# A two-layer hybrid attention and mLSTM inference step on one core: the order of the work set anew, and eight two-input operations on the other of VectorE and GpSimd

## Chip, cores and metric

One core of one Trainium2 chip runs the whole step. The metric is the device time of one execution in microseconds (us), lower is better; the kernel before takes 915.91 us (median of 3 runs, 913.62 to 922.15).

## The reference, cut to what matters

560 tokens (32 of a sample stream, 16 meta tokens, 512 of a prompt) go through two layers. All is in float32. Per layer:

```python
h = rmsnorm(x, norm_g)
q, k, v, z_a, qi, ki, wi, u, v_m, o_m, z_m, ig, fg = split_cols(h @ w_in)
q, k = rope(rmsnorm(q)), rope(rmsnorm(k))                # 8 heads x 64
score = (relu(qi.ki) * wi).sum(heads); keep the top 128  # sparse attention
attn = softmax(q.k of the kept keys) @ v
c = silu(causal_conv(u)); qm, km = c @ wq_m, c @ wk_m    # mLSTM, 4 heads x 128
num, den = mlstm_chunks(qm, km, v_m, ig, log_sigmoid(fg))
h_m = rmsnorm(num / den)
mixed = [attn * silu(z_a), (sigmoid(o_m) * h_m + skip * c) * silu(z_m)]
y = x + mixed @ w_out
```

Results are `y`, the keys, values and indexer keys of both streams, and the mLSTM and conv states.

## The kernel before, in words

Activations lie with features on the partitions and the 560 tokens along the free axis, cut in two halves of 304 and 256 (`HALVES`). Each weight piece (128 or 256 columns wide) is loaded in 256 KB parts by `load_piece` (L498) and split into a high and a low part (`whi` by ScalarE, L472; `wlo = wraw - whi`, L509); the activations are split likewise, and every product is three TensorE matmuls: high by high (L554), low by high (L555), high by low (L556) in `mm_feat`, and the same in `mm_tok` (L531 to L533). So a 128-wide projection is 48 matmuls. PSUM has four pools of two buffers each: `pj` for projections, `sc`, `tp` and `pv` for the rest. A third projection half can therefore start only when the drain of the first (the instruction that reads PSUM) is done. A drain has a priority of its own, stage "D".

The work of a layer is a list of steps, each a letter and an index:

- I and the KI piece (the head of `layer`): indexer queries and keys; J ropes and splits the indexer key (`rope` L599 to L607; splits at L713, L714). R ropes and splits the indexer queries (`stack_split` L564, its subtraction is L569), X0 to X3 (`index_pair`, matmuls L765) and N (`index_sample`, L789, L793) make the scores, T0 to T3 (`top`) find the top 128 with max and match_replace on VectorE (L821, L822).
- U0 to U3 (`conv`): projection, drains L889 to L891 on VectorE, convolution. M0, M1: the mLSTM's values. E: gates. F0 to F4 (`ml_front`, L929 to L946), C0 to C4 (`ml_mid`, L958 to L974, each after the one before), B0 to B4 (`ml_back`): the mLSTM by chunks of tokens.
- Q0 to Q3, K0 to K3 (`qk`): projection, rope, the sums of squares (L1030), a chain of small operations on GpSimd for the reciprocal root (`rsqrt` L580, L586 to L591; L1040), and for K a transpose on TensorE (L1049), a trip through DRAM (`kscr`), a scaling (L1059) and the split (L569). V0, V1 (`proj_v`): attention values. Apj (`attend`; Ap4 is `attend_last`): attention of head pair p for token block j, with scores L1166, transposes L1183 and L1192, values L1200. It needs Qp, Kp, both V and, for block j, the masks of T.
- O, Z, G (`gate_o`, `gate_z`): gates, with drains L1218 and L1238. S0 to S7 (`split`, subtraction L1253): split of the mixed features. Y0 to Y7: output projection; in layer 0 it also makes layer 1's split input and its sum of squares (`take` L615, the add is L634). `norm` (L639) turns the sums into `rrow`, with which every drain multiplies.

What an engine runs is set by a scheduler: every instruction has a priority, the ready instruction with the lowest goes first, and the compiled program then runs in that fixed order on each engine. A step's priority is

```python
off[0] = 500 * OPT[f"pos{l}"] * i + 10000 * SHIFT[l].get(t, 0)
with prio(l * 1000000 + PR[l][stage] + off[0]): ...
```

where `i` is the step's position in `STEPS[l]`. `OPT` names, per place and layer, the engine of an operation: `E(site, l)` is VectorE for 0 and GpSimd for 1. All DMAs are issued by SyncE.

Of the kernel before, what the change touches and what calls it, by code (L numbers as in the profile page):

```python
# [53 lines left out]
for _n in WORDER:  # L54
# [47 lines left out]
       'S': 138000,
       'Y': 633000},
      {'Q': 25000,
       'n': 189000,
       'I': 479000,
       'J': 576000,
       'R': 22000,
       'X': 516000,
       'N': 264000,  # L110
       'T': 267000,
       'E': 394000,
       'D': 325000,
       'U': 576000,
       'M': 397000,
       'F': 244000,
       'C': 244000,
       'B': 336000,
       'K': 420000,
       'V': 331000,  # L120
       'A': 22000,
       'O': 509000,
       'Z': 647000,
       'G': 559000,
       'S': 241000,
       'Y': 217000}]
# [6 lines left out]
          'V0': 1,  # L133
          'V1': 15,
          'S3': -3,
          'X3': 4,
          'S5': -3,
          'Z1': 31,
          'U3': -10,
          'M0': 5,  # L140
          'Y3': -20,
          'O3': -10,
          'A14': -2,
          'C4': 10,
          'T0': 23,
          'Y1': 10,
          'A04': 8,
          'A03': -7,
          'A02': 62,
          'A01': 4,  # L150
          'A10': -49,
          'A22': 1,
          'A34': -13,
          'A31': 38,
          'A30': -20,
          'Y4': -23,
          'Y6': -10,
          'Y7': -20,
          'T1': -2,
          'B1': -10,  # L160
          'N': -14,
          'G1': -13,
          'A23': -38,
          'A11': 20,
          'A13': 10,
          'A24': -8,
          'A20': -10,
          'A33': -15,
          'Y0': -5,
          'F4': 43,  # L170
          'F0': 47,
          'F1': 40,
          'C0': 10,
          'F2': -29,
          'X2': -1,
          'O1': -3,
          'S6': -6,
          'Q1': 3,
          'O2': -4,
# [1241 lines left out]
```

## Time and profile before

| | |
|---|---|
| median of 3 runs | 915.91 us (913.62 to 922.15) |
| the profiled execution | 916.5 us, of which the span of its records is 914.4 us |
| mean granted clock of TensorE | 0.966 of full speed |
| PE, VectorE, ScalarE, GpSimd busy | 842.5, 671.5, 481.4, 315.9 us |
| layer 0 / layer 1 | about 0 to 465 / 465 to 914 us (layer 1's sums end at 464.6) |

The engines are called PE (TensorE), DVE (VectorE), ACT (ScalarE) and POOL (GpSimd) in the profile. "Idle before" an instruction is the time in which its engine had nothing running, and the arrow names what was waited for. Matmuls overlap, so a row's own duration is longer than its step to the next row.

### The profile page before, as it was taken

To read this page: it belongs to the slowest core of one execution; us is meant where nothing else is said; L and a number is where in the kernel's file an instruction comes from. 1 tells how busy PE (TensorE), PEld (TensorE's weight loads), DVE (VectorE), ACT (ScalarE), POOL (GpSimd) and SP (SyncE) were. 2 spreads that over 40 slices of the span, in tenths; PEclk is the share of its full clock that TensorE was granted. 3 is DMA by queue.
4 is the path that set the end of the run, shared out by engine and by line. 5 is a ranking of instruction groups with operands and counts; after the bars stand their busy time and mean duration, and the time that the engine had idled before them with its cause. 6 is when DMAs were issued, how large, how long until landed. Compare 5 with 4: busy or idle time off the path is not lost.

```text
span 914.4 us, 18487 instructions
## 1 busy us (share of the span) xinstructions
PE 842.5 (92%) x6582; PEld 794.2 (87%) x6582; DVE 671.5 (73%) x1659; ACT 481.4 (53%) x1231; POOL 315.9 (35%) x562
## 2 busy tenths in 40 slices
PE   5978799999989999998999889998998989999998
PEld 4978589889979989878999778998998878989998
DVE  7699988899986674674438997899999745655531
ACT  6255625565537645565534565563664755465520
POOL 6162200374501123443714300284776121451111
PEclk9997889999999999999999899998899999989999
DMA  6433214353463333423633332254257313341252
GB/s 206 121 104 80 74 49 118 101 152 96 133 190 96 96 106 83 134 70 105 203 95 96 91 94 84 72 143 106 62 167 228 102 43 92 105 115 48 65 181 70
DMA packets 82155, 99.96 MB, mean 109 GB/s; under 512 B 16720, under 2 KB 44192, under 8 KB 82064
## 3 DMA queue, kind: packets, MB, share of 16 engines
q1 hardware_dynamic: 82064, 98.79, 38.1%
q8 instruction: 51, 0.84, 0.4%
q14 instruction: 40, 0.33, 0.1%
HBM read 72.19 MB, written 15.21 MB: 96 GB/s over the span
## 4 chain that ended last, share of the span: by engine, by line
PE 49%; DVE 22%; DMA 10%; ACT 6%; issue 5%; SPq 4%; POOL 3%; DVEq 0%; POOLq 0%; ACTq 0%
PE pj L554 10%; PE pj L556 10%; PE pj L555 10%; SPq L486 4%; DVE wk L822 3%; PE pv L1200 2%; DVE m L821 2%; DVE wlo L509 2%; PE sc L1166 2%; DMA fx<-fr 2%; DMA fx<-kscr 2%; PE tp L1183 1%; DMA kscr<-rows 1%; DMA fx<-tok 1%; PE pj L533 1%
## 5 line engine op out<-in xcount | busy, mean ns | idle before, releaser
L554 PE MATMUL pj<-h,whi 128*128 128x304 f32 (+3 forms) x548 | 165.7, 305 | 21.7 <-DVE gt L890 9.6
L472 ACT ACTIVATE whi<-wraw 128x512 fp32r<-128x512 f32 x180 | 111.9, 626 | 127.0 <-PE pj L556 95.6
L556 PE MATMUL pj<-h,whi 128*128 128x304 f32 (+3 forms) x548 | 164.2, 302 | 5.7 <-DVE h L624 5.7
L555 PE MATMUL pj<-h,wlo 128*128 128x304 f32 (+3 forms) x548 | 163.9, 300 | 0.0
L509 DVE TENSOR_TENSOR wlo<-wraw,whi 128x512 fp32r<-128x512 f32 x136 | 104.8, 773 | 36.6 <-ACT whi L472 35.9
L554 PEld LDWEIGHTS pj<-h,whi 128*128 128x128 f32 (+1 forms) x548 | 106.4, 195 | 25.1 <-issue 9.9
L556 PEld LDWEIGHTS pj<-h,whi 128*128 128x128 f32 (+1 forms) x548 | 105.6, 193 | 9.2 <-DVE h L624 8.4
L554 PE MATMUL pj<-at,whi 128*128 128x304 f32 (+2 forms) x346 | 105.9, 306 | 8.1 <-DVE gt L890 4.3
L555 PEld LDWEIGHTS pj<-h,wlo 128*128 128x128 f32 (+1 forms) x548 | 106.8, 195 | 0.6 <-issue 0.3
L555 PE MATMUL pj<-at,wlo 128*128 128x304 f32 (+2 forms) x346 | 104.2, 302 | 0.0
L556 PE MATMUL pj<-at,whi 128*128 128x304 f32 (+2 forms) x346 | 103.5, 300 | 0.0
L509 POOL TENSOR_TENSOR wlo<-wraw,whi 128x512 fp32r<-128x512 f32 x44 | 58.1, 1322 | 113.0 <-ACT whi L472 111.1
L554 PEld LDWEIGHTS pj<-at,whi 128*128 128x128 f32 (+1 forms) x346 | 67.3, 195 | 9.8 <-issue 4.4
L821 DVE MAX8 m<-wk 96x8 f32<-96x560 f32 (+3 forms) x120 | 67.6, 563 | 1.8
L555 PEld LDWEIGHTS pj<-at,wlo 128*128 128x128 f32 (+1 forms) x346 | 67.5, 195 | 0.1
L556 PEld LDWEIGHTS pj<-at,whi 128*128 128x128 f32 (+1 forms) x346 | 67.6, 195 | 0.0
L822 DVE MATCH_REPLACE8 wk<-m,wk 96x560 f32<-96x560 f32 (+3 forms) x120 | 65.8, 548 | 0.0
L605 POOL TENSOR_TENSOR fx<-fx,sinT 128x560 f32<-128x560 f32 (+1 forms) x17 | 27.1, 1594 | 86.6 <-DMA fx<-fr 86.5
L554 PE MATMUL pj<-tok,whi 128*128 128x304 f32 (+3 forms) x188 | 56.7, 301 | 0.0
L555 PE MATMUL pj<-tok,wlo 128*128 128x304 f32 (+3 forms) x188 | 55.9, 297 | 0.0
L556 PE MATMUL pj<-tok,whi 128*128 128x304 f32 (+3 forms) x188 | 55.7, 296 | 0.0
L1176 ACT ACTIVATE lg<-lg,sta,ssq 128x176 f32<-128x176 f32 (+3 forms) x64 | 43.8, 686 | 20.4 <-DVE sta L1174 19.9
(369 smaller groups left out, 2349.7 us busy)
## 6 DMA issues: line engine op xcount, KB each, us to landing
wraw<-w SPq DMA_DIRECT2D x176, 256.0 KB
fx<-fr SPq DMA_DIRECT2D x68, 70.0 KB
m<-scratch SPq DMA_DIRECT2D x16, 256.0 KB
fx<-tok SPq DMA_DIRECT2D x32, 70.0 KB
c2scr<-ca SPq DMA_DIRECT2D x8, 280.0 KB
k_out<-fr SPq DMA_DIRECT2D x8, 280.0 KB
gt<-c2scr SPq DMA_DIRECT2D x8, 280.0 KB
m<-hmscr SPq DMA_DIRECT2D x8, 280.0 KB
```

What stands on the lines that cost most here:

```text
L472: return act.activation(out, in_, AF.Copy, scale=scale)
L486: return nc.sync.dma_start(out, in_)
L509: (gps if o == 2 or (o == 1 and q % 2) else dve).tensor_tensor(lo, raw, hi.bitcast(F32), op=OP.subtract)
L554: pe.matmul(o, wh, hh, start=(i == 0 and j == 0), stop=False)
L555: pe.matmul(o, wl, hh, start=False, stop=False)
L556: pe.matmul(o, wh, hl, start=False, stop=(i == 1 and j == 3))
L605: E(f"r{site}a", l).tensor_tensor(rot, rot, sinT[:32 * n], op=OP.mult)
L821: dve.max(m8[:R], src)
L822: dve.match_replace(out=wk[:R, :S], in_to_replace=m8[:R], in_values=src, imm_value=NEG)
L1166: pe.matmul(ps[:R, :n], qq[p][t][s][:, c0:c0 + R], kk[p][s][:, a:a + n], start=(t == 0), stop=(t == 1))
L1176: act.activation(lgs[s][:R, :S], lgs[s][:R, :S], AF.Exp, bias=nb[:, s:s + 1], scale=ssq[:R, p, j, s:s + 1], accum_out=den[:, s:s + 1])
L1200: pe.matmul(pv[64 * s:64 * s + 64, 0:R], v[:, hs], pr, start=(i < 0), stop=(i == j))
```

## The change

No instruction of the body is altered. The tables `PR` (stage priorities), `SHIFT` (step shifts), `STEPS` and `OPT` are set anew; the tables are longer, so each body line has a number that is 14 higher after (L1049 is L1063). Cut to its core:

```diff
 PR = [{...
-       'J': 383000,    'R': 196000,  'X': 309000,  'D': 141000,
-       'C': 309000,    'B': 483000,  'S': 138000,
+  'J': 401276,  'R': 20000,  'X': 131603,  'D': 90115,
+  'C': 328696,  'B': 195945,  'S': 137917,
...
       {...
-       'I': 479000,  'J': 576000,  'X': 516000,  'N': 264000,  'T': 267000,  'D': 325000,
-       'C': 244000,  'B': 336000,  'K': 420000,  'V': 331000,  'Z': 647000,  'Y': 217000}]
+ 'I': 360837,  'J': 730646,  'X': 133061,  'N': 359859,  'T': 71421,  'D': 353929,
+ 'C': 20000,  'B': 311969,  'K': 386914,  'V': 307457,  'Z': 600664,  'Y': 391429}]
 OPT = {...
-       'skb11': 1,  'rJa0': 1,  'rKb1': 0,  'rQc1': 1,  'tb0': 1,  'kb00': 0,  'sq00': 0,  'sq10': 1,
+ 'skb11': 0,  'rJa0': 0,  'rKb1': 1,  'rQc1': 0,  'tb0': 0,  'kb00': 1,  'sq00': 1,  'sq10': 0,
 STEPS (layer 1)
-    ... C3 B0 K1 V0 V1 ... T1 A04 A02 O2 A03 A14 A12 A10 A01 A00 ... A24 A20 A21 Q3 ... K3 ... A30 S7 A31 A33 A32 ...
+    ... C3 V0 B0 K1 V1 ... T1 A03 A04 A02 O2 A14 A12 A10 A00 ... A13 A01 ... A20 A24 A21 Q3 K3 ... A30 A34 S7 A33 A31 A32 ...
```

Of the shifts, those of layer 1 set C3 from 29 to -26, G1 from -5 to -27, Z2 from 1 to -31, A01 to 37 and A33 to -41, among others. The eight flipped operations, by the line numbers of before:

- from GpSimd to VectorE: the fourteen adds L634 of layer 0's input, the first rope product L605 of layer 0's indexer key (one), the splits L1253 of S4 to S7 in layer 0, the last rope add L607 of Q0 to Q3 in layer 1, and the second half of the split L569 of K0 to K3 in layer 1;
- from VectorE to GpSimd: two of layer 0's four subtractions L714, the splits L1253 of S0 to S3 in layer 0, and the second rope product L606 of K0 to K3 in layer 1.

What stands on VectorE in layer 0 ahead of and behind the drain of the first conv step (U1: L889 and L890; L714 belongs to J, L605, L607 and L569 on `fx`, `tok`, `at` to the indexer queries), before:

```order
L714 TENSOR_TENSOR at_601<-fr_296,at_600 64x560
L482 CAST at_602<-lg_604 64x512
L869 MEMSET m_15_1435 4x16
L605 TENSOR_TENSOR fx_749<-fx_749,sinT_238 128x560
L714 TENSOR_TENSOR at_603<-lg_604,at_602 64x512
L607 TENSOR_TENSOR tok_350<-tok_350,fx_749 128x560
L569 TENSOR_TENSOR at_680<-tok_297,at_680 64x560
L889 TENSOR_TENSOR gt_955<-pj_958,rrow_423 128x32
L890 TENSOR_TENSOR gt_955<-pj_958,rrow_423 128x272
L569 TENSOR_TENSOR at_681<-tok_297,at_681 64x560
```

and after (L903 and L904 are the drain; L743 to L749 are the copies of the indexer weights, `wx` and `wsel`):

```order
L583 TENSOR_TENSOR at_681<-tok_297,at_681 64x560
L743 COPY wx_639<-tp_625 128x24
L523 TENSOR_TENSOR wlo_1030<-wraw_1028,whi_1029 128x512
L621 TENSOR_TENSOR tok_350<-tok_350,fx_749 128x560
L746 COPY wx_639<-tp_625 64x4 x2
L749 TENSOR_SCALAR wsel_643<-blk_1_71,tp_625 128x32 x2
L619 TENSOR_TENSOR fx_814<-fx_814,sinT_238 128x560
L523 TENSOR_TENSOR wlo_1103<-wraw_1101,whi_1102 128x512
L583 TENSOR_TENSOR at_746<-tok_350,at_746 64x560
L583 TENSOR_TENSOR at_747<-tok_350,at_747 64x560
L903 TENSOR_TENSOR gt_955<-pj_958,rrow_423 128x32
L904 TENSOR_TENSOR gt_955<-pj_958,rrow_423 128x272
```

The two subtractions L714 have gone from VectorE, and indexer-query work that stood behind the drain (L605 on `fx_814`, the splits into `at_681`, `at_746`, `at_747`) now stands ahead of it; on PE twelve score matmuls of X0 now stand between the two conv steps.

On PE in layer 1, from K0's transpose (L1049) on, before, with V0's first matmuls (L528) at the end:

```order
L1049 MATMUL tp_8138<-ident_68,smk_8121 10x128
L1030 MATMUL tp_8242<-blk_70,lg_8179 128x2 x5
L929 MATMUL tp_8291<-ca_6565,pt_6111 128x128 x4
L929 MATMUL tp_8298<-ca_6565,pt_6112 128x128 x4
L936 MATMUL tp_8305<-ident_68,m_101_8303 128x128 x4
L945 MATMUL sc_8312<-m_100_8296,m_101_8303 128x128 x4
L968 MATMUL pv_8333<-tok_7466,m_96_8002 128x129 x2
...
L1116 MATMUL sc_9278<-h_8158,qz_2_6540 128x280
L528 MATMUL pj_8607<-whi_8582,hc_5592 112x256
L528 MATMUL pj_8607<-wlo_8583,hc_5592 48x256 x2
```

and after, around the same transpose (L1063; L545 to L547 are V0's matmuls by token blocks, `pj_8482` and `pj_8509`):

```order
L547 MATMUL pj_8482<-whi_8422,tok_5458 128x256
L545 MATMUL pj_8482<-whi_8428,tok_5459 128x256
L546 MATMUL pj_8482<-wlo_8429,tok_5459 128x256
L547 MATMUL pj_8482<-whi_8428,tok_5460 128x256
L545 MATMUL pj_8482<-whi_8428,tok_5461 128x256
L546 MATMUL pj_8482<-wlo_8429,tok_5461 128x256
L547 MATMUL pj_8482<-whi_8428,tok_5462 128x256
L1063 MATMUL tp_8138<-ident_68,smk_8121 10x128
L545 MATMUL pj_8509<-whi_8410,at_5447 128x256
L546 MATMUL pj_8509<-wlo_8411,at_5447 128x256
L547 MATMUL pj_8509<-whi_8410,at_5448 128x256
```

V0's token projections, which came behind the whole of that stretch, now stand in front of and behind the transpose, and the 48 of K1's projection stand among F3 and C2 a little later.

On PE in layer 1, K3's transpose L1049 (`tp_10207`) before:

```order
L556 MATMUL pj_10361<-tok_5462,whi_10353 128x256
L1049 MATMUL tp_10207<-ident_68,smk_10190 10x128
L1183 MATMUL tp_10320<-ident_68,lg_10305 128x128 x2
L554 MATMUL pj_10557<-at_5447,whi_10544 128x304
L555 MATMUL pj_10557<-at_5447,wlo_10545 128x304
```

and K3's transpose after (L1063 on `tp_10631`; `pj_10987` is a gate projection, L1197 a transpose of A23):

```order
L569 MATMUL pj_10987<-tok_5461,wlo_10980 128x256
L570 MATMUL pj_10987<-tok_5462,whi_10979 128x256
L1063 MATMUL tp_10631<-ident_68,smk_10614 10x128
L1197 MATMUL tp_10823<-ident_68,lg_10799 128x128 x4
L568 MATMUL pj_11290<-at_5447,whi_11277 128x304
L569 MATMUL pj_11290<-at_5447,wlo_11278 128x304
```

Where the transpose was row 4591 of 5415 on PE, it is row 4893 of 5428; the first score matmul of A3 (L1180, `sc_139`) follows 85 rows behind it, and the attention steps A30 to A34, which were spread over the Z, G and first Y projections, stand close together.

## Rows read from the trace of the kernel before

**Rows 1.** the page: busy us of engines (part 1), clock per slice (part 2)
```profile
PE 842.5 (92%) x6582; PEld 794.2 (87%) x6582; DVE 671.5 (73%) x1659; ACT 481.4 (53%) x1231; POOL 315.9 (35%) x562
...
PEclk9997889999999999999999899998899999989999
```

**Rows 2.** busy time by stretch: us, engines' busy us (count), clock, DMA share, GB/s
```profile
0.00:40.00 40.00, 28.86 (x153) 25.83 (x154) 26.33 (x50) 18.77 (x50) 17.22 (x40) 1.00 0.59 177
40.00:120.00 80.00, 63.22 (x419) 57.07 (x418) 74.91 (x129) 43.87 (x102) 26.84 (x26) 0.85 0.31 82
...
500.00:570.00 70.00, 62.52 (x437) 57.72 (x436) 63.89 (x122) 44.04 (x105) 10.51 (x16) 0.95 0.34 91
570.00:700.00 130.00, 122.38 (x934) 116.31 (x934) 120.30 (x297) 70.75 (x201) 77.90 (x185) 0.95 0.44 120
700.00:820.00 120.00, 110.26 (x876) 101.93 (x875) 73.31 (x211) 66.07 (x168) 40.49 (x70) 0.93 0.36 102
```

**Rows 3.** waits of PE over the span: tile, line, releaser; us, times, longest
```profile
PE pj L554 <- DVE gt L890: 13.8, 3, 9.6
```

**Rows 4.** timeline of PE, layer 0, first conv step: start, us, operation [idle before]
```profile
72.05 0.59 PE L554 MATMUL pj<-h,whi 128*128 128x304 f32 x1 [9.56 <-DVE gt L890]
```

**Rows 5.** timeline of VectorE over the same stretch
```profile
65.32 1.87 DVE L605 TENSOR_TENSOR fx<-fx,sinT 128x560 f32<-128x560 f32 x1
67.12 1.75 DVE L714 TENSOR_TENSOR at<-lg,at 64x512 fp32r<-64x512 f32 x1
...
69.55 1.79 DVE L569 TENSOR_TENSOR at<-tok,at 64x560 fp32r<-64x560 f32 x1
...
71.48 0.43 DVE L890 TENSOR_TENSOR gt<-pj,rrow 128x272 f32<-128x272 f32 x1
```

**Rows 6.** timeline of PE at the sample's indexer scores, layer 0
```profile
112.88 0.83 PE L789 MATMUL pv<-at,at 128*128 128x280 f32 x2 [2.45 <-ACT lg L769]
```

**Rows 7.** timeline of PE, layer 1, first conv step
```profile
509.12 0.59 PE L554 MATMUL pj<-at,whi 128*128 128x304 f32 x1 [4.03 <-DVE gt L890]
```

**Rows 8.** timeline of PE, layer 1, around K0's row transpose
```profile
631.99 0.39 PE L1049 MATMUL tp<-ident,smk 128*10 128x128 f32 x2 [1.72 <-POOL smk L1040]
...
640.25 2.09 PE L968 MATMUL pv<-tok,m 128*128 128x129 f32 x8 [0.54 <-ACT m L472]
...
647.45 0.42 PE L528 MATMUL pj<-whi,hc 128*112 128x256 f32 x1
```

**Rows 9.** busy time by stretch: both places, the second's surroundings, layer 0's tail
```profile
62.00:80.00 18.00, 8.44 (x44) 8.26 (x43) 17.69 (x28) 8.74 (x22) 9.98 (x7) 0.62 0.48 117
630.00:648.00 18.00, 14.49 (x74) 13.16 (x73) 16.18 (x46) 9.12 (x27) 9.93 (x28) 0.63 0.33 93
600.00:700.00 100.00, 92.38 (x697) 88.58 (x696) 93.34 (x237) 57.14 (x164) 67.75 (x171) 0.93 0.46 126
393.00:423.00 30.00, 25.97 (x239) 21.70 (x238) 15.80 (x54) 16.40 (x46) 7.92 (x21) 1.00 0.14 41
```

**Rows 10.** timeline of PE, layer 1, K3's row transpose
```profile
788.77 0.39 PE L1049 MATMUL tp<-ident,smk 128*10 128x128 f32 x2
```

**Rows 11.** timeline of VectorE, layer 1, K3's scaling and first split
```profile
796.07 1.45 DVE L1059 TENSOR_TENSOR fr<-fr,fx 128x560 f32<-128x560 f32 x1 [2.20 <-DMA fx<-kscr]
...
798.25 0.73 DVE L569 TENSOR_TENSOR h<-fr,h 64x560 fp32r<-64x560 f32 x1 [0.33 <-ACT h L472]
```

**Rows 12.** single lines: engine, operation xcount: ns min/median/max, first and last start
```profile
L631 DVE TENSOR_TENSOR lg<-m x14: 410/468/1104, 5.6 to 25.8; 128x304 f32<-128x304 f32 x7, 128x256 f32<-128x256 f32 x7
...
L606 POOL TENSOR_TENSOR fr<-fr,cosT x10: 1367/1400/1886, 54.5 to 808.3; 128x560 f32<-128x560 f32 x8, 64x560 f32<-64x560 f32 x2
...
L606 DVE TENSOR_TENSOR fr<-fr,cosT x8: 741/836/1997, 172.9 to 780.5; 128x560 f32<-128x560 f32 x8
...
L607 DVE TENSOR_TENSOR tok<-tok,fx x8: 704/728/742, 58.4 to 524.9; 128x560 f32<-128x560 f32 x8
...
L569 DVE TENSOR_TENSOR h<-fr,h x4: 734/735/736, 644.9 to 798.3; 64x560 fp32r<-64x560 f32 x4
```

More of the change, by code (lines that the diff above doesn't have):

```diff
@@ L132 @@
 SHIFT = [{'S1': 17,
[L133 to L179, printed above, removed]
@@ new lines @@
+  'V1': 15,
+  'S3': -3,
+  'X3': 4,
+  'S5': -1,
+  'Z1': 31,
+  'U3': -10,
+  'M0': 5,
+  'Y3': -20,
+  'O3': 1,
+  'A14': -2,
+  'C4': 10,
+  'T0': 23,
+  'Y1': 10,
+  'A04': -11,
+  'A03': -7,
+  'A02': 62,
+  'A01': -22,
+  'A10': -49,
+  'A22': 1,
+  'A34': -13,
+  'A31': 38,
+  'A30': -20,
+  'Y4': -23,
+  'Y6': -10,
+  'Y7': -20,
+  'T1': -2,
+  'B1': -10,
+  'N': -14,
+  'G1': 1,
+  'A23': -38,
+  'A11': 20,
+  'A13': 10,
+  'A24': -8,
+  'A20': -10,
+  'A33': -15,
+  'Y0': -5,
+  'F4': 43,
@@ new lines @@
+  'F0': 47,
+  'F1': 40,
+  'C0': 10,
+  'F2': -29,
+  'X2': 26,
+  'O1': -3,
+  'S6': -6,
+  'Q1': 3,
+  'O2': -4,
+  'U1': -10,
+  'X1': 3,
+  'A21': -3,
+  'B3': -5,
+  'O0': -2,
+  'T3': -27,
+  'A00': 8,
+  'Y2': -44,
+  'K2': -19,
+  'B4': -35},
+ {'G3': -5,
+  'S1': 2,
+  'U1': -2,
+  'O0': 22,
+  'O2': 50,
+  'O1': 3,
+  'O3': 39,
+  'U2': 3,
+  'S6': 2,
+  'S7': -5,
+  'S4': 12,
+  'S3': 2,
+  'C4': 18,
+  'G1': -27,
+  'B2': 3,
+  'F4': -2,
+  'F3': -12,
+  'E': 47,
+  'V0': -12,
+  'A10': 3,
+  'Y2': 10,
+  'Z1': -2,
+  'M0': -5,
+  'Z3': -3,
+  'B1': -13,
+  'K2': -1,
+  'A14': 1,
+  'G2': -5,
+  'Z2': -31,
+  'X1': -23,
+  'M1': 16,
+  'C2': -9,
+  'Z0': -5,
+  'C3': -26,
+  'B4': -2,
+  'Q1': 14,
+  'Q2': 5,
+  'Q3': -16,
+  'N': -45,
+  'F1': -4,
+  'F2': -24,
+  'T1': 2,
+  'T3': 40,
+  'K3': -1,
+  'C0': 50,
+  'A31': -7,
+  'V1': 5,
+  'A21': 18,
+  'A33': -41,
+  'A01': 37,
+  'B3': -10,
+  'A04': -4,
+  'A22': -9}]
@@ new lines @@
+ 'wlU0': 0,
+ 'wlU1': 0,
+ 'whM0': 0,
+ 'whM1': 0,
+ 'wlM0': 0,
+ 'wlM1': 0,
+ 'whQ0': 0,
+ 'whQ1': 0,
+ 'wlQ0': 0,
+ 'wlQ1': 0,
+ 'whV0': 0,
+ 'whV1': 0,
+ 'wlV0': 0,
+ 'wlV1': 0,
+ 'whO0': 0,
+ 'whO1': 0,
+ 'wlO0': 1,
+ 'wlO1': 2,
+ 'whZ0': 0,
+ 'whZ1': 0,
+ 'wlZ0': 0,
+ 'wlZ1': 0,
+ 'whG0': 0,
+ 'whG1': 0,
+ 'wlG0': 1,
+ 'wlG1': 1,
+ 'whY0': 0,
+ 'whY1': 0,
+ 'wlY0': 2,
+ 'wlY1': 1,
+ 'sca0': 0,
+ 'sca1': 0,
+ 'scb0': 0,
+ 'scb1': 0,
+ 'sia00': 0,
+ 'sQa00': 0,
+ 'ska00': 0,
+ 'sib00': 0,
+ 'sQb00': 0,
@@ new lines @@
+ 'rQa0': 1,
+ 'rQa1': 1,
+ 'rQb0': 0,
+ 'rQb1': 1,
+ 'rQc0': 1,
+ 'rQc1': 0,
+ 'ta0': 0,
+ 'ta1': 0,
+ 'tb0': 0,
+ 'tb1': 1,
+ 'tc0': 1,
+ 'tc1': 0,
+ 'td0': 0,
+ 'td1': 1,
+ 'ie0': 0,
+ 'ie1': 0,
+ 'ka00': 1,
+ 'ka01': 1,
+ 'kb00': 1,
+ 'kb01': 0,
+ 'ka10': 0,
+ 'ka11': 0,
+ 'kb10': 1,
+ 'kb11': 1,
+ 'xr000': 0,
+ 'xr001': 0,
+ 'xr010': 0,
+ 'xr011': 0,
+ 'xr100': 0,
+ 'xr101': 0,
+ 'xr110': 0,
+ 'xr111': 0,
+ 'xr200': 0,
+ 'xr201': 0,
+ 'xr210': 0,
+ 'xr211': 0,
+ 'xr300': 0,
+ 'xr301': 0,
+ 'xr310': 0,
@@ L413 @@
     """
[L414 to L416 removed]
+    X0 X1 X2 X3 U0 U2 N U3 U1 E F4 F0 T3 M0 M1 Q0 C4 F1 B4 T0 C0 F2 C1 K0 Q1 F3 C2 B2 C3 V0 B0 K1 V1 Q2 B1 B3 O1
+    T2 T1 A03 A04 A02 O2 A14 A12 A10 A00 O0 K2 O3 Z3 A13 A01 Z0 A11 Z1 A20 A24 A21 Q3 K3 Z2 G0 A23 A22 G2 G1 A30
```

420 lines of the change are left out of this document (146 added, 274 removed).

## Prediction

> **What bounds the kernel now.** The page's busy times come first: TensorE is busy 842.5 of the span of 914.4 us, VectorE 671.5 [rows 1]. So 72 us of the span have no matmul, and a second loss lies inside the busy time: the slices of the clock line that stand below full speed [rows 1]. The table by stretches then says where both are [rows 2]. In 0 to 40 us TensorE is busy 28.86: the start, with its loads. In 40 to 120 it is busy 63.22 of 80 at a mean clock of 0.85, which is 24 us at the half level (1.2 GHz). Layer 1 loses 7.5 us idle in 500 to 570, 7.6 in 570 to 700 and 9.7 in 700 to 820, with clocks of 0.95, 0.95 and 0.93, that is 7, 13 and 17 us at the half level. The stretches that I left out of these rows run at full clock and lose less. So what a new order can give back is some 17 + 25 us of idle time in these stretches, and half of the 61 us at half clock. It cannot shorten the 842.5 us of matmuls otherwise, because no matmul is removed.
>
> The waits of TensorE name the largest single cause: drain L890 of a conv step, 13.8 us in 3 waits, of which one is 9.6 [rows 3]. From here I read the timeline at the four places where the new order differs most on the engines that wait or are waited for.
>
> **The change part by part.** The sum is made against the profiled execution of 916.5 us (span 914.4 and 2.1 around it), 0.6 above the median of 915.9.
>
> *Place A, layer 0, 62 to 120 us.* U0's first matmul waits 9.56 us for U1's drain L890 [rows 4], and the clock is at its half level in much of the stretch around it: 62 to 80 us has 0.62 and TensorE busy only 8.44 of 18, 8 of it after the wait at the half level [rows 9]. VectorE is late with the drain because it stands behind a row of subtractions and rope products that take 1.75 to 1.87 us each, where the same forms take 0.73 when GpSimd is quiet [rows 5, 12]. After, two L714 are gone from VectorE (1.75 for one, for the other I take the quiet 0.73, together 2.5), but an L605 and three L569 stand ahead of the drain that stood behind it (4 x 0.74 = 3.0, by the quiet duration in [rows 12]). The drain itself comes no sooner: 0.5 us later. What helps is on TensorE: twelve score matmuls of X0 stand between the two conv steps and fill some 3 to 4 us of the 9.56. But 40 to 120 has VectorE at 74.91 of 80 [rows 2], so the work that TensorE does early is mostly paid back at the next wait for the same engine: the sample's scores wait 2.45 us at 112.88 [rows 6], and U2 still stands behind them. I credit 3 us. Bounds: -14 (the wait's 9.6 and half of those 8 us), if wait and half clock vanish; +5, if the drain moves later by its displaced 3.0 and the clock stays down twice.
>
> *Start, the fourteen adds L634.* The nearest VectorE row is L631 on the same tiles, 0.41 to 1.10, median 0.47 [rows 12]. 14 x 0.47 = 6.6 us more for VectorE, in a stretch where it is busy 26.33 of 40 [rows 2]; the loads hide them. Against that the add no longer changes engines. I take 0, bounds -2 and +3 (norm then comes behind the KI matmuls).
>
> *Place B, layer 1, 509 us.* U0's third half waits 4.03 us for L890 [rows 7]. Five small copies and products for the indexer weights go behind that drain on VectorE; I take a quarter of the wait: -1, bounds -4 (wait gone) and 0.
>
> *Place C, layer 1, 630 to 648 us, the main term.* K0's transpose L1049 waits for the GpSimd chain of the reciprocal root, then only small matmuls follow: F3 (L929 on), C2 and C3 (L968 and L958, waiting for ScalarE and VectorE), until V0 begins at 647.45 [rows 8]. In these 18 us TensorE is busy 14.49 and the clock is 0.63, which is 13.3 us at the half level [rows 9]. After, V0's token projections stand ahead of and behind the transpose and K1's 48 matmuls among F3 and C2, so the chains run beside dense work. Gain: the 3.5 us idle, and of the 13.3 us at half clock the busy four fifths (14.49/18), 10.7 us, halved: 5.4. Together 9. It holds only if VectorE does not become the next bound: in 600 to 700 it is busy 93.34 of 100 [rows 9]. What stands on VectorE ahead of O1's gate at the end of that stretch is unchanged within 0.5 us, but the max and match_replace rounds of T1 and T2 now precede C2's and C3's updates. Bounds -13 (the waits behind it too) and +4.
>
> *Place E, layer 1, 700 to 820.* A03, A02 and A14 move in among V1, Q2, O1 and O2, A01 behind O3 and Z3. The stretch loses 9.7 us idle and 17 us at half clock [rows 2], 18 us altogether with half of the latter. I credit a quarter, rounded down, -4, since the attention steps bring waits of their own to where they go; bounds -9 and +4.
>
> *Place D, layer 1, the tail.* K3's transpose stood at 788.77 [rows 10]; its rows went through DRAM, the scaling began at 796.07 and the first split at 798.25 [rows 11], so some 11 us from transpose to usable keys. After, it is row 4893 of TensorE instead of 4591 and A30's first score stands 85 rows behind, which at 842.5/6582 = 0.128 us each, the mean over all matmuls [rows 1], is 10.9 us: just about enough. The attention steps of pair 3 then stand close together with few projections between. The nearest row for such a dense tail is layer 0's own, 393 to 423, with 25.97 busy of 30, 4 us lost [rows 9]. Part of such a loss is there in layer 1 now; I take +2.5, bounds 0 and +9 (the chain late by several us and the 4 us on top).
>
> *The other operations moved.* In layer 1 VectorE receives Q's four L607 (4 x 0.73) and K's four L569 (4 x 0.735) and gives up K's four L606 (4 x 0.84, the median): +2.5 us [rows 12]. Half of these fall where VectorE is nearly full, so +1; S0 to S3 on GpSimd in layer 0 take 1.40 in place of 0.73 us, by other forms of the same size [rows 12], the last of them ahead of the first output matmuls: +0.5. Together +1.5, bounds -3 and +4.
>
> That VectorE and GpSimd disturb each other is in the rows: L606 on VectorE takes 0.74 to 2.0 us, and its GpSimd form 1.37 to 1.89 [rows 12]. The Trainium skill, page "SBUF — State Buffer", section "SBUF: two separate sides", says that the two share a port pair as an exclusive lock, held for a whole instruction, against two-input VectorE operations. By that rule K's L606 on GpSimd frees VectorE of nothing: it would cost 4 x (1.40 - 0.84) = 2.2 us where it meets such an operation, while the eight that leave GpSimd would give 8 x (1.40 - 0.73) = 5.4. The sum by the rule would be up to some 5 us lower than with my +1.5 for this term; the spread of L606's durations agrees that some of them block, but not all.
>
> Sum: A -3, start 0, B -1, C -9, E -4, D +2.5, operations +1.5, which is -13: 903.5 for a profiled execution, 903 beside the median of 915.9.
>
> **The rivals.** *VectorE takes the place of the wait (no change).* In 600 to 700 VectorE has 6.7 us free in 100 [rows 9]; with T1 and T2 ahead of C2 and C3, TensorE runs V0 early and then waits for the drains and updates behind them. C's 9 comes back; with A -3, B -1 and E and D at about 0, and +1.5 for the operations, the sum is -2: 914. For it: the share, and the wait for a VectorE drain, which is the largest group [rows 3]. Against: L1049's own wait and the first 6 us of the half clock hang on GpSimd and ScalarE, not on it.
>
> *The late K3 chain decides (slower).* The 85 rows between K3's transpose and A30 cover 10.9 us; the chain took 11 with VectorE idle 2.20 us before L1059 [rows 11]. If rows or splits queue behind gates there, or the stages before run 3 us faster than the loads, all of A30 to A34 stand without cover, at layer 0's rate of loss for 30 us (4) and at half clock for some 13 us (6), and pair 3's gate and split follow late. With that +10 and C given back as above plus VectorE's top work in front of C3 (+4), the sum is -3 -1 +10 +4 +1.5 = +11.5: 927. It decides from a chain of some 14 us on. Against it: a dense tail in layer 0 costs only 4.
>
> *The start stall vanishes too.* If the twelve matmuls keep the clock up in place A, the half-level time behind the wait goes as well, 4 us, and 3 more of the wait: -7, 896. Against: 5 to 6 us of wait remain.
>
> **How the numbers follow.** Forecast 903 with its own range 896 to 911: chance 0.48. VectorE as bound, 914: 0.25. K3's chain, 927: 0.17. Start too, 896: 0.10. A measurement of this kernel can tell about 1% (9.2 us) from no change, so the bounds are 906.7 and 925.1. Three quarters of the forecast (0.36) and the last rival (0.10) are faster: 0.46. A quarter of the forecast (0.12) and VectorE as bound (0.25) are within: 0.37. The K3 rival is slower: 0.17. The range reaches to 889 (the forecast with 7 us from the start and 7 from C and E's lower bounds) and to 924, short of the K3 case.
>
> **What would show it.** In the changed profile: the wait for U1's drain (L904) should fall from 9.6 to about 6; the stretch that holds K0's transpose (L1063) should have a clock near 1 and TensorE over 95% busy; C3's matmuls should not wait more than 1 us each for VectorE; A30's first score should wait under 2 us for K3's split; the last stretch from S to the end should be unchanged. The prediction is wrong if waits for VectorE over 3 us stand between 600 and 720, or if a half-clock spell stands in A30 to A34.

## The result and the profile after

The changed kernel takes 891.53 us (median of 3 runs, 889.6 to 891.58) against 915.91: 24.4 us less, a ratio of 0.9741 with a 95% interval of 0.9697 to 0.9786. The forecast was 903 us with a range of 889 to 924. The direction was right and the time lies in the range, 2.5 us from its lower end; the gain is nearly twice the forecast one, and several terms are not where I had put them.

The body's lines have numbers that are 14 higher in the profile after. The page of the changed kernel, as in [rows 1]:

```profile
span 887.8 us, 18458 instructions
...
PE 828.6 (93%) x6582; PEld 783.7 (88%) x6582; DVE 661.8 (75%) x1675; ACT 480.9 (54%) x1231; POOL 295.2 (33%) x546
...
PEclk9889999999999999999999989999999999999999
```

The span is 26.6 us shorter. The same 6582 matmuls are busy for 828.6 us instead of 842.5, 13.9 us less, and since no matmul was removed this is mostly the clock, 0.982 in the mean where before has 0.966; TensorE's idle time fell from 71.9 (914.4 - 842.5) to 59.2 (887.8 - 828.6), which is the other 12.7. VectorE has 16 more instructions and is yet busy 9.7 us less.

The share of the clock is the less certain of the two. In the 61 further executions of the kernel before, beside the experiments below, the mean clock lay between 0.961 and 0.981, about 0.97 in the middle, so the 0.966 of the page is a low one. Three kernels below are no faster than before; in their traces TensorE was busy 842.0, 840.6 and 838.4 us. Against these the changed kernel's 828.6 is 10 to 13 us less.

The table by stretches of the changed kernel, with the stretches of [rows 2] (start and end, us, busy us of each engine with the count of its instructions, granted clock, DMA share, GB/s), and one more:

```profile
0.00:40.00 40.00, 28.33 (x170) 25.82 (x171) 28.77 (x74) 19.67 (x52) 4.57 (x27) 0.96 0.64 190
40.00:120.00 80.00, 65.99 (x462) 62.09 (x462) 73.52 (x135) 43.53 (x102) 27.72 (x29) 0.93 0.29 76
...
500.00:570.00 70.00, 64.52 (x450) 59.74 (x450) 64.68 (x125) 39.40 (x99) 9.35 (x16) 0.93 0.29 79
570.00:700.00 130.00, 125.19 (x988) 120.60 (x986) 118.24 (x316) 73.69 (x208) 76.14 (x194) 0.99 0.44 124
700.00:820.00 120.00, 117.75 (x1009) 110.81 (x1009) 73.90 (x201) 72.73 (x180) 38.47 (x66) 1.00 0.39 112
820.00:880.00 60.00, 56.52 (x475) 52.99 (x474) 22.16 (x73) 21.07 (x50) 7.72 (x6) 1.00 0.34 106
```

The last stretch of the kernel before:

```profile
820.00:880.00 60.00, 58.57 (x514) 56.20 (x512) 30.77 (x88) 29.66 (x69) 10.88 (x14) 1.00 0.24 69
```

As both kernels run the same matmuls, the counts tell where the lead is won, at 0.128 us for a mean matmul. In 0 to 120 us the changed kernel runs 632 matmuls where before ran 572: 60 more, about 7.7 us. In 500 to 570 it is 13 more (1.7 us), in 570 to 700 54 more (6.9 us), in 700 to 820 133 more (17 us), and in 820 to 880 39 fewer (-5 us). So the largest gain is in the stretch that I had credited with 4 us. Between 120 and 500 us, which the table leaves out, the changed kernel runs 19 fewer, so a part of the early lead is given back; but layer 0's tail within it, to which the prediction gave no term, has 25 more (3.2 us). Before, then changed:

```profile
380.00:440.00 60.00, 54.24 (x462) 48.86 (x461) 34.78 (x91) 36.40 (x96) 29.27 (x39) 1.00 0.35 105
```

```profile
380.00:440.00 60.00, 58.18 (x487) 53.48 (x486) 33.01 (x84) 38.09 (x98) 34.32 (x46) 1.00 0.45 129
```

(The count is a measure of progress, no exact sum: long and short matmuls count alike, and the later stretches hold different work.)

The waits of TensorE, as in [rows 3]: the group that led before, the conv drain (L904 now), is down to 1.8 and 2.9 us at most. The longest that leads now is a new one, 5.5 us for a projection's drain on ScalarE.

```profile
PE pj L568 <- ACT tok L486: 6.2, 2, 5.5
...
PE pj L568 <- DVE gt L904: 3.5, 3, 1.8
PE pj L542 <- DVE gt L904: 2.9, 1, 2.9
```

Place A of the prediction, 62 to 80 us, by the table of stretches of the changed kernel; [rows 9] has 8.44 busy, 44 matmuls and a clock of 0.62 for it:

```profile
62.00:80.00 18.00, 15.86 (x109) 15.21 (x109) 17.50 (x28) 10.02 (x29) 7.33 (x10) 0.94 0.32 77
```

This stretch alone shows too much. The new wait stands just ahead of it, and the 22 us in front of it run 124 matmuls where the kernel before ran 181. The changed kernel:

```profile
60.52 0.62 PE L568 MATMUL pj<-h,whi 128*128 128x304 f32 x1 [5.53 <-ACT tok L486]
```

```profile
40.00:62.00 22.00, 16.47 (x124) 16.06 (x124) 18.83 (x30) 10.33 (x18) 13.58 (x9) 0.81 0.31 78
```

So the 9.56 us wait did not vanish: TensorE now waits 5.53 us before the stretch, and the matmuls that follow that wait run at the half level, until 64 us. What is left over 0 to 120 us also depends on the execution. Four kernels below (V0 early, layer 1, rear, front) run the matmuls of layer 0 in before's order, line by line and tile by tile, and ran 585, 616, 616 and 616 in that time. Before, the layer 1 kernel, and the changed kernel:

```profile
0.00:120.00 120.00, 92.08 (x570) 82.90 (x571) 101.24 (x179) 62.63 (x152) 44.06 (x66) 0.90 0.40 114
```

```profile
0.00:120.00 120.00, 94.34 (x616) 86.39 (x616) 100.99 (x185) 63.53 (x154) 50.16 (x68) 0.96 0.40 114
```

```profile
0.00:120.00 120.00, 94.32 (x630) 87.91 (x631) 102.29 (x208) 63.20 (x154) 32.29 (x55) 0.94 0.41 114
```

The four other kernels with the changed order in layer 0 ran 624 to 633. By the means of five and five, 601 and 628, the lead at 120 us is 27 matmuls, some 3.5 us; the 7.7 against the page of before contain its low clock.

Place C, around K0's transpose, now at 625.74 with no wait noted before it, and behind it the stretch with the small matmuls (timeline and stretches of the changed kernel):

```profile
625.74 0.39 PE L1063 MATMUL tp<-ident,smk 128*10 128x128 f32 x2
```

```profile
612.00:632.00 20.00, 20.00 (x170) 19.54 (x170) 18.41 (x59) 8.03 (x20) 10.51 (x21) 1.00 0.23 60
632.00:650.00 18.00, 15.38 (x111) 14.88 (x110) 16.84 (x34) 10.29 (x26) 7.23 (x14) 0.91 0.49 147
```

Around the transpose TensorE is busy all of 20 us at full clock. Part of the hole has moved to 632 to 650, where F3 and C2 are: 2.6 us idle and a clock of 0.91, against 3.5 and 0.63 in [rows 9].

Place D, the tail of layer 1 in the changed kernel: K3's transpose and the first scores of A30 on TensorE, the scaling and the first split on VectorE, and the stretches of the dense tail.

```profile
805.75 0.39 PE L1063 MATMUL tp<-ident,smk 128*10 128x128 f32 x2
...
818.29 0.40 PE L1180 MATMUL sc<-h,h 128*128 128x256 f32 x2
```

```profile
814.75 0.74 DVE L1073 TENSOR_TENSOR fr<-fr,fx 128x560 f32<-128x560 f32 x1 [1.97 <-DMA fx<-kscr]
...
816.89 1.50 DVE L583 TENSOR_TENSOR h<-fr,h 64x560 fp32r<-64x560 f32 x2
```

```profile
816.00:830.00 14.00, 12.98 (x125) 11.80 (x124) 11.48 (x44) 11.12 (x31) 1.28 (x1) 1.00 0.34 99
830.00:842.00 12.00, 9.54 (x90) 7.19 (x89) 4.56 (x17) 7.57 (x21) 0.00 (x0) 1.00 0.00 1
```

The chain from the transpose to the end of the split takes 12.6 us and A30's scores start right with its end, without a wait: the cover is just enough. What the dense tail loses is 3.5 us idle in 816 to 842, at full clock.

### The profile page after: what moved, and what is told of

Same layout as the page of the kernel before. It is cut to its first block, busy times and chain, and to the rows that moved or that the text cites. A ratio compares the mean times of both kernels' runs of the same rounds, so it can differ in the third digit from the quotient of the medians.

```text
span 887.8 us, 18458 instructions
## 1 busy us (share of the span) xinstructions
PE 828.6 (93%) x6582; PEld 783.7 (88%) x6582; DVE 661.8 (75%) x1675; ACT 480.9 (54%) x1231; POOL 295.2 (33%) x546
## 4 chain that ended last, share of the span: by engine, by line
PE 46%; DVE 27%; DMA 8%; ACT 6%; issue 6%; SPq 3%; POOL 3%; DVEq 0%; ACTq 0%; POOLq 0%
PE pj L568 10%; PE pj L570 9%; PE pj L569 9%; DVE wk L836 4%; DVE wlo L523 3%; SPq L500 3%; DVE m L835 3%; PE pv L1214 2%; PE sc L1180 2%; ACT lg L1190 1%; DMA fx<-fr 1%; PE pj L546 1%; DMA fx<-kscr 1%; PE pj L547 1%; PE pj L545 1%
## 5 line engine op out<-in xcount | busy, mean ns | idle before, releaser
L569 PE MATMUL pj<-h,wlo 128*128 128x304 f32 (+3 forms) x548 | 163.4, 299 | 0.0
L523 DVE TENSOR_TENSOR wlo<-wraw,whi 128x512 fp32r<-128x512 f32 x136 | 100.4, 741 | 41.0 <-ACT whi L486 40.6
L568 PE MATMUL pj<-at,whi 128*128 128x304 f32 (+2 forms) x346 | 104.2, 302 | 6.9 <-DVE gt L904 2.5
L569 PEld LDWEIGHTS pj<-h,wlo 128*128 128x128 f32 (+1 forms) x548 | 106.0, 193 | 0.7 <-issue 0.3
L570 PE MATMUL pj<-at,whi 128*128 128x304 f32 (+2 forms) x346 | 102.9, 298 | 0.0
L569 PE MATMUL pj<-at,wlo 128*128 128x304 f32 (+2 forms) x346 | 102.6, 297 | 0.0
L568 PEld LDWEIGHTS pj<-at,whi 128*128 128x128 f32 (+1 forms) x346 | 66.3, 192 | 8.4 <-DVE gt L1232 2.1
L619 POOL TENSOR_TENSOR fx<-fx,sinT 128x560 f32<-128x560 f32 x16 | 25.8, 1612 | 132.7 <-DMA fx<-fr 117.1
L570 PEld LDWEIGHTS pj<-at,whi 128*128 128x128 f32 (+1 forms) x346 | 66.3, 192 | 0.2 <-issue 0.2
L569 PEld LDWEIGHTS pj<-at,wlo 128*128 128x128 f32 (+1 forms) x346 | 66.3, 192 | 0.0
L569 PE MATMUL pj<-tok,wlo 128*128 128x304 f32 (+3 forms) x188 | 55.9, 297 | 0.0
```

The costliest lines, as they stand in the source:

```text
L523: (gps if o == 2 or (o == 1 and q % 2) else dve).tensor_tensor(lo, raw, hi.bitcast(F32), op=OP.subtract)
L568: pe.matmul(o, wh, hh, start=(i == 0 and j == 0), stop=False)
L569: pe.matmul(o, wl, hh, start=False, stop=False)
L570: pe.matmul(o, wh, hl, start=False, stop=(i == 1 and j == 3))
L619: E(f"r{site}a", l).tensor_tensor(rot, rot, sinT[:32 * n], op=OP.mult)
```

## The experiments

Theory 1 at the outset was the prediction's: the order makes the gain, place by place. All kernels here keep before's line numbers. Ratios are to the kernel before, with 95% intervals; the changed kernel has 0.9741 (0.9697 to 0.9786).

**The eight flips alone, the order tables alone.**

```diff
# flips_only: before's PR, SHIFT, STEPS
-'skb11': 1, 'rJa0': 1, 'rKb1': 0, 'rQc1': 1, 'tb0': 1, 'kb00': 0, 'sq00': 0, 'sq10': 1
+'skb11': 0, 'rJa0': 0, 'rKb1': 1, 'rQc1': 0, 'tb0': 0, 'kb00': 1, 'sq00': 1, 'sq10': 0
# order_only: the changed PR, SHIFT, STEPS, with the first of these two lines
```

> Before's order tables, with only the eight operations flipped. Theory 1 (the order alone makes the gain): 913 to 919 us, within 0.4% of before. Theory 2 (the flips take VectorE and GpSimd out of each other's way, and VectorE's busy time, which fell from 671.5 to 661.8 us in the changed kernel, falls through them): 908 us or less, with VectorE busy 8 to 10 us less.

> The changed kernel's order tables, with the eight operations on before's engines. Theory 1 (order): 889 to 895 us. Theory 2 (flips): 899 us or more, VectorE busy about 670 us.

Flips alone: 906.34 us where before was 912.7, ratio 0.9925 (0.9896 to 0.9955). Order alone: 905.42, ratio 0.992 (0.9889 to 0.9951). Both theories fall in their plain form: each half gives some 7 us, and the product of the two, 0.9845, is short of the 0.9741 by 1%, outside the change's interval. The order and the flips need each other. The times that had been expected of the second theory, 908 us or less and 899 or more, were met by both kernels, though VectorE's busy time fell by 6.1 us with the flips alone and not by the 8 to 10 expected: the flips do carry a part of the gain.

Place A shows what the flips do. The stretch 62 to 80 us, first with the flips alone, then with the order alone:

```profile
62.00:80.00 18.00, 15.89 (x108) 15.15 (x108) 17.55 (x29) 10.01 (x29) 7.62 (x10) 0.94 0.32 76
```

```profile
62.00:80.00 18.00, 9.82 (x56) 9.85 (x57) 17.66 (x28) 9.38 (x25) 10.05 (x7) 0.72 0.45 113
```

and the wait for the conv drain with the order alone, up to 130 us:

```profile
PE pj L554 <- DVE gt L890: 8.6, 1, 8.6
```

With the flips alone the stretch is that of the changed kernel (108 matmuls, 0.94; the changed one has 109, 0.94). With the order alone the 9.6 us wait is still 8.6. A flipped operation becomes ready for the scheduler at another time, so the order behind it is sorted anew, also on TensorE, which runs none of the flipped operations: this is the part of an `OPT` entry that the diff doesn't tell. In the flips-only kernel TensorE's order is, line by line, that of the changed kernel up to 79 us, and leaves before's order at 15 us. So the X0 matmuls that moved in between the conv steps, on which my term A rested, come from the flips, and so does the new wait ahead of the stretch, 5.63 us here.

**The layers apart.**

```diff
# layer0_only: PR[0], SHIFT[0], STEPS[0] and the flips tb0, rJa0, kb00, sq00, sq10 as changed; layer 1 as before
# layer1_only: PR[1], SHIFT[1], STEPS[1] and the flips skb11, rKb1, rQc1 as changed; layer 0 as before
```

> The changed tables and flips of layer 0, those of before for layer 1. At equal work done the changed trace is 8.2 us ahead at the end of layer 0. Theory 1 (the layers' gains add): 906 to 909 us. Rival (the lead is taken back at layer 1's first wait, which hangs on VectorE): 912 us or more.

> The changed tables and flips of layer 1, those of before for layer 0. At equal work done layer 1 gains 18.4 us of the 26.6. Theory 1 (the layers' gains add): 896 to 900 us. Rival (layer 1's gain depends on what layer 0 leaves): 904 us or more.

Layer 0: 906.34 us, ratio 0.9927 (0.9894 to 0.996). Layer 1: 898.65 us, ratio 0.9841 (0.9805 to 0.9877). Their product is 0.9769, inside the change's interval: the layers' gains add, as theory 1 had it, some 7 us and 14.5. That doesn't show that flips and order need each other only within a layer: the kernel with layer 1's flips back, below, speaks against it.

**Layer 0's flips one by one.**

```diff
# tb0_only, on before:            # jk0_only, on before:
-'tb0': 1                         -'kb00': 0, 'rJa0': 1
+'tb0': 0                         +'kb00': 1, 'rJa0': 0
```

> Before's tables, with the fourteen adds L634 of layer 0 on VectorE and nothing else. Theory 1 (the adds, on the engine that makes their input, are what the 6 us lead of layer 0 comes from): 904 to 908 us by the time scale of the first four runs (before 912.7), the wait for drain L890 in layer 0 well under 9.6 us. Theory 2 (J's operations make it, since L714 and L605 stood ahead of the drain): within 2 us of before.

> Before's tables, with two L714 on GpSimd and the L605 of kraw on VectorE, nothing else. Theory 1 (the adds): within 2 us of before, the wait for L890 still 8 us or more. Theory 2 (J's operations): 904 to 908 us where before is 912.7.

The adds alone: 914.79 us where before was 913.64, ratio 1.0004 (0.9968 to 1.004). J's operations alone: 914.39, ratio 1.0024 (0.9994 to 1.0055). Neither gives the time, and both expectations of a gain miss. The adds alone do take the drain's wait away (none over 2.6 us is left up to 130 us), but a new one for a split of the indexer queries stands there; the stretch 62 to 80 has 85 matmuls, between before's 44 and the 108 of all flips. The waits up to 130 us, and the stretch:

```profile
PE pv L765 <- DVE at L569: 3.0, 1, 3.0
PE pj L528 <- DVE gt L890: 2.6, 1, 2.6
```

```profile
62.00:80.00 18.00, 13.44 (x85) 12.97 (x85) 17.52 (x28) 8.58 (x26) 7.32 (x10) 0.86 0.29 72
```

J's operations alone leave the wait at 7.4:

```profile
PE pj L554 <- DVE gt L890: 7.4, 1, 7.4
```

But with the adds alone TensorE also waits 5.05 us for ScalarE ahead of this stretch, and over 0 to 120 us it runs 616 matmuls, as many as three of the kernels with before's order; up to 465 us it falls 5 behind the kernel before. J's operations alone run 561 in 0 to 120, all eight flips 629. So neither group makes the lead by itself. That the two together make it is likely, as the other flips stand later in the program, but it was not run, nor were the flips of S0 to S7 alone or the five of layer 0 without layer 1's three on before's tables.

**V0 early, alone.**

```diff
# v0_early, on before, STEPS of layer 1:
-... C3 B0 K1 V0 V1 ...
+... C3 V0 B0 K1 V1 ...
```

> Before, with V0 moved ahead of B0 and K1 in layer 1's list and nothing else, so that its weights load ahead of K1's. Theory 1 (V0's dense matmuls beside the K0 chain are worth 6 to 9 us by themselves): 904 to 908 us where before is 912.7, the clock of the stretch with K0's transpose near 1. Rival (VectorE is the bound of 570 to 700, so what comes early is waited for later): within 2 us of before, with new waits for VectorE before 720 us.

916.05 us where before was 913.64, ratio 1.0031 (0.9993 to 1.0069): nothing, as the rival had it. The trace shows where the lead goes. The stretches 612 to 640 and 640 to 690 us of before, then of this kernel:

```profile
612.00:640.00 28.00, 25.01 (x189) 23.66 (x187) 25.87 (x79) 12.50 (x34) 13.73 (x34) 0.90 0.39 99
640.00:690.00 50.00, 48.77 (x369) 47.51 (x370) 47.74 (x121) 31.52 (x98) 36.51 (x101) 0.92 0.41 116
```

```profile
612.00:640.00 28.00, 24.52 (x208) 24.24 (x206) 26.87 (x84) 10.86 (x26) 8.44 (x20) 0.99 0.34 89
640.00:690.00 50.00, 43.01 (x291) 40.45 (x290) 43.95 (x108) 28.14 (x88) 35.88 (x96) 0.88 0.39 112
```

19 matmuls more by 640, 78 fewer in the 50 us behind it. The long waits there, from this kernel's timeline of TensorE:

```profile
639.80 0.60 PE L1049 MATMUL tp<-ident,smk 128*10 128x128 f32 x2 [3.48 <-POOL smk L1040]
...
652.29 0.49 PE L958 MATMUL pv<-tok,m 128*128 128x129 f32 x2 [2.11 <-DVE cnp L974]
```

The dense work is used up by 640 us, with VectorE busy 26.87 of the 28 us before, and K0's chain, 8 us later than before, stands uncovered again. The rival was right on the time, but only half right on the engine: the 3.48 us hang on GpSimd's chain, the 2.11 on VectorE.

**C and T back.** With V0 early in the changed kernel, the priorities of the mLSTM's updates and of top-k go back:

```diff
# ct_back, on the changed kernel, layer 1
-PR 'C': 20000, 'T': 71421    SHIFT 'C0': 50, 'C3': -26, 'T1': 2
+PR 'C': 244000, 'T': 267000  SHIFT 'C3': 29, 'T1': -5
```

> The changed kernel with the priorities of C and T and the shifts of C0, C3 and T1 as before; V0 still early. Theory 1 (V0 early pays only when the top-k and the mLSTM's updates are pulled ahead too, which is why V0 alone gave nothing): 6 us or more slower than the changed kernel, 0.981 of before or more, the loss between 640 and 720 us. Rival (V0's own gain is lost in the old list for another reason): within 2 us of the changed kernel, 0.972 to 0.977.

896.21 us where before was 916.35, ratio 0.9784 (0.9736 to 0.9832). The step from 0.9741 is 4 us, less than the 6 expected, and the two intervals overlap, so the times alone don't settle it. The place agrees with theory 1: in 640 to 690 this kernel runs 326 matmuls at a clock of 0.93, the changed one 381 at 0.97, and one of the mLSTM's updates waits 5.61 us, for ScalarE. The stretch and the wait in this kernel, then the stretch in the changed one:

```profile
640.00:690.00 50.00, 43.05 (x326) 42.09 (x326) 45.73 (x130) 33.53 (x103) 36.03 (x103) 0.93 0.44 129
```

```profile
646.27 1.23 PE L968 MATMUL pv<-tok,m 128*128 128x129 f32 x4 [5.61 <-ACT m L472]
```

```profile
640.00:690.00 50.00, 48.94 (x381) 48.14 (x381) 47.22 (x146) 30.39 (x96) 39.29 (x116) 0.97 0.43 124
```

**Layer 1's flips back.**

```diff
# l1flips_back, on the changed kernel
-'skb11': 0, 'rKb1': 1, 'rQc1': 0
+'skb11': 1, 'rKb1': 0, 'rQc1': 1
```

> The changed kernel with the three operations of layer 1 (L607 of Q, L606 and the second L569 of K) on before's engines. Theory 1 (the order makes layer 1's gain): within 2 us of the changed kernel, 0.974 of before. Rival (the flips and the order need each other, as the first four runs add to 14 us where the change has 24): 5 us or more slower than the changed kernel, 0.980 of before or more.

894.25 us where before was 913.64, ratio 0.9787 (0.9733 to 0.9841): 4 us above the changed kernel's 0.9741, between the two expectations, with intervals that overlap. Its trace has 977 matmuls in 700 to 820 us where the changed one has 1009. Nothing here speaks for the cost that I had put on the flips of layer 1; whether they gain, and how much, stays open.

This kernel differs from the one with the order alone by layer 0's five flips and nothing else, and there the intervals do not overlap: 0.9787 (0.9733 to 0.9841) against 0.992 (0.9889 to 0.9951), some 12 us, 6 to 18 by the intervals. So layer 0's flips at least are what the order needs. They also reach into layer 1: the two kernels have the same tables and engines there, and yet their orders on TensorE part at 530 to 537 us. Through which operation is open.

**Front and rear of layer 1.**

```diff
# both on before, with the flips skb11, rKb1, rQc1
# rear_only: STEPS[1] from O1 on, PR[1] K, Z, Y, SHIFT[1] of A, G, Z as changed
# front_only: STEPS[1] up to B3, PR[1] I, J, X, N, T, D, C, B, V, the other SHIFT[1] as changed
```

> Before's layer 0 and the front part of layer 1 (up to B3 in the list); from O1 on the changed list, with the changed priorities of K, Z and Y, the changed shifts of A, G and Z, and layer 1's three flips. Theory 1 (the 12 to 15 us that the changed trace wins between 700 and 840 us of the old time come from the rear tables alone): 0.990 of before or less, that is 8 us or more after the tail's loss of 5. Rival (the rear can only use what the front part delivers early): 0.995 or more.

> Before's layer 0 and the rear part of layer 1; the changed front part (priorities I, J, X, N, T, D, C, B, V, their shifts and the list up to B3) with layer 1's three flips. Theory 1 (front and rear add to layer 1's 0.984): 0.992 to 0.996. Rival (the front carries the whole): 0.984 to 0.988.

Rear: 904.04 us where before was 916.35, ratio 0.987 (0.9819 to 0.992). Front: 908.72, ratio 0.9934 (0.9898 to 0.997). Theory 1 holds on both: the rear brings its 12 us without the front, and 0.987 x 0.9934 = 0.9805 is at the edge of layer 1's 0.9841 (0.9805 to 0.9877). (Both carry layer 1's flips, so whatever these give is counted twice in the product.) The stretch 700 to 820 us of the rear kernel:

```profile
700.00:820.00 120.00, 117.20 (x982) 110.97 (x981) 73.54 (x214) 68.73 (x171) 40.67 (x77) 0.99 0.37 104
```

982 matmuls against before's 876: attention steps of pairs 0 to 2 stand among more projections. In the changed kernel 115 of the 133 further matmuls of this stretch are projections, and all sixteen drains of the Z and G gates (L1252) begin by 817 us, where before had eight of its sixteen (L1238).

The clock, 0.99 against 0.93, tells less than it seems to. Two half-clock spells of before (774 to 782, 801 to 809) are gone in the changed kernel; but they are also gone in the kernel with the adds alone, which runs layer 1 on TensorE in before's order, line by line. Before, changed, and the adds alone:

```profile
774.00:782.00 8.00, 7.34 (x38) 7.09 (x37) 4.55 (x16) 3.10 (x8) 3.77 (x9) 0.57 0.25 71
801.00:809.00 8.00, 6.59 (x36) 5.94 (x33) 2.36 (x10) 3.88 (x12) 2.02 (x2) 0.57 0.49 138
```

```profile
774.00:782.00 8.00, 8.00 (x69) 7.67 (x69) 5.47 (x17) 3.94 (x10) 6.09 (x13) 1.00 0.48 122
801.00:809.00 8.00, 8.00 (x63) 7.65 (x62) 2.35 (x5) 2.20 (x6) 4.17 (x7) 1.00 0.33 100
```

```profile
774.00:782.00 8.00, 7.34 (x58) 7.04 (x57) 5.04 (x18) 5.12 (x13) 2.23 (x8) 1.00 0.25 71
801.00:809.00 8.00, 6.55 (x59) 5.61 (x58) 3.84 (x14) 5.34 (x18) 1.17 (x2) 1.00 0.59 171
```

What the kernels with the old rear list share is idle time: over 700 to 820 us TensorE is busy 107 to 110 us in before, adds, J, V0, front, layer 0 and flips, which run 869 to 908 matmuls at clocks of 0.93 to 1.00 there. The rear kernel is busy 117.20, the changed one 117.75.

**K3 earlier, an attempt to beat both kernels.**

```diff
# k3_early, on the changed kernel, STEPS of layer 1
-... A01 Z0 A11 Z1 A20 A24 A21 Q3 K3 Z2 ...
+... A01 K3 Z0 A11 Z1 A20 A24 A21 Q3 Z2 ...
```

> The changed kernel with K3 in front of Z0 in layer 1's list, so that A30 to A34 find projections beside them. Theory 1 (the 4 to 5 us that the changed trace loses between 816 and 842 us are the price of the dense tail): 886 to 889 us by the first time scale, 0.968 to 0.971 of before. Rival (the projections that K3 takes with it are missing beside A2): 0.974 or more.

891.62 us where before was 916.35, ratio 0.9736 (0.9695 to 0.9777): the same as the changed kernel, so neither expectation is excluded but no gain is seen. The trace shows a trade. The tail is mended, but 7 us at the half level stand in front of it, in this execution:

```profile
776.00:790.00 14.00, 12.10 (x107) 11.12 (x106) 7.23 (x17) 7.14 (x19) 3.98 (x3) 1.00 0.43 123
790.00:797.00 7.00, 7.00 (x36) 6.33 (x36) 5.81 (x17) 4.74 (x13) 2.03 (x8) 0.52 0.60 162
797.00:850.00 53.00, 52.28 (x461) 49.43 (x461) 28.73 (x88) 29.30 (x70) 9.60 (x16) 1.00 0.18 51
```

0.7 us idle in the 53 us that hold the tail, where the changed kernel loses 3.5 in 26; in return 1.9 us idle in 776 to 790 and half of 7 us. Theory 1's reading of the tail holds. The trace fits the rival too: only 8 of the matmuls in 790 to 797 are projections, where the changed kernel has 54. One trace can't say that the half level there belongs to the order.

## Why the prediction was right, and where its steps failed

- *What bounds it.* Right: what a new order gave back was TensorE's idle time (12.7 us) and busy time at the half level (13.9 between the two pages). By the mean clocks, 0.966 and 0.982, the half-level time fell from about 62 us (914.4 x 0.034 x 2) to 32. What I missed is that the half-level spells of one trace are in part that execution's own: I took their places for the order's.
- *Place A (-3).* Given to the wrong edit. 0 to 120 us gained 7.7 by the count against the page of before, some 3.5 by the means of five executions of each order, so the size was not bad. My step "what helps is on TensorE: twelve score matmuls of X0" saw the right move, but took it as the order's. The order alone leaves the wait at 8.6 us; the flips make the move. The rival "the start stall vanishes too" did not come: the 5.53 us wait for ScalarE is new, and the first dozen matmuls behind it run at the half level. And one reading was wrong: the sample's scores in [rows 6] wait for ScalarE and not, as I wrote, for VectorE again.
- *Layer 0's tail (no term).* I showed its 4 us of loss in [rows 9] as a neighbour for place D and credited nothing there. 380 to 440 us has 25 matmuls more, 3 us; the four kernels with before's order of layer 0 ran 464 to 468 there, the four others with the changed one 487 to 492. With place A that is near the layer 0 kernel's 7 us.
- *Start (0).* The step "the loads hide them" is right as far as it goes: the adds alone are 1.0004. That they sort the order behind them anew, with a wait of 5 us for ScalarE at 60 us, was missing.
- *Place B (-1).* 500 to 570 has 13 matmuls more, about 1.7 us, and its clock fell from 0.95 to 0.93. Small, as said.
- *Place C (-9, "the main term").* Around 612 to 690 the changed kernel runs 601 matmuls where before ran 558: 43 more, 5.5 us. Mis-sized, and my step from V0's early projections to the gain was too short: V0 early alone is worth nothing. Its time is that of the rival "VectorE takes the place of the wait", though the longer of the new waits hangs on GpSimd. In the changed kernel no wait for VectorE over 1 us is left in 600 to 720 us, as the sign that I had set asks.
- *Place E (-4).* This is the step that failed most: "I credit a quarter". 700 to 820 has 133 matmuls more (17 us) than the page of before and 101 to 140 more (13 to 18 us) than the kernels with the old rear list; the rear tables alone are worth 12 us net of the tail, beyond my bound of -9. The 9.7 us of idle time fell to 2.3, because the Z and G projections moved in beside the attention steps; I had looked only at where the attention steps went.
- *Place D (+2.5).* The right mechanism, and about the right size: idle time in 820 to 880 rose from 1.4 to 3.5 us, 2 us more; by the count it is 39 matmuls fewer (5 us), but the stretch holds other work in the two kernels. The rows of layer 0's tail were a good neighbour (4 us in 30). The chain was covered, as worked out: 12.5 us from the transpose to A30's scores; the slower rival did not happen, and no half-clock spell stands in the tail.
- *The operations (+1.5).* Not shown either way: the flips of layer 1 taken back cost 4 us, within the noise, and those of S0 to S7 were not run alone. All eight flips gave 7 us, though VectorE carries 16 instructions more; how much of that is this term's is open. VectorE's busy time fell by 6 us with the flips alone (671.5 to 665.4 on the page) and by 1.2 with the order alone (to 670.3). One reason stands in the row of L631 in the flips-only kernel, beside which the adds ran on GpSimd before (its longest was 1104 ns in [rows 12]):

```profile
L631 DVE TENSOR_TENSOR lg<-m x14: 409/440/476, 6.1 to 25.1; 128x304 f32<-128x304 f32 x7, 128x256 f32<-128x256 f32 x7
```

None takes over 476 ns any more. In the kernel with the adds alone VectorE carries these fourteen adds, 6 us, and is busy as long as before, 671.5 us: its other operations became shorter by as much. By the rule of the Trainium skill that the prediction weighed ("SBUF — State Buffer", section "SBUF: two separate sides"), a GpSimd operation and a two-input VectorE operation share an exclusive lock, and the one that starts first holds up the other. The trace agrees here. But the adds alone shorten L631 just so and the time stays at 1.0004: less blocking is not yet time.

The sum came out too small by 11 us. E was short by 8 to 13 and layer 0's tail by 3, against C, which was 3.5 too good; A, B and D were near. What the operations gave is not known. That 891.5 lies in the range is in part luck: I had its lower end from 7 us at the start and 7 from the bounds of C and E, but C gave less than its term and E more than its bound.

## What to carry to other kernels

Where a scheduler sorts the instructions, an operation that changes its engine moves the order behind it too, so look at the new order of every edit by itself before giving a gain to one of them. Dense work that is pulled beside a chain can be used up before the chain ends; then the hole moves behind it, as V0 alone showed. Count the matmuls by stretch in both traces, also in the stretch in front of the one that got better, and credit a stretch by its whole idle time when projections come to stand in it. Read a place's clock in more than one execution of the same order before you price it.
